# Two more weight-chunk slots from a halved DMA scratch, and conditioning chunks taken two at a time

## The chip, the cores and the metric

The kernel runs on one core of one Trainium2 chip. The metric is the device time of one execution in microseconds. Several executions of each kernel are taken on the same chip; their median stands for the kernel. One further execution was recorded by the hardware profiler, and all rows below come from it.

## The reference

One layer of a hybrid decoder trunk (D = 2048), for 256 prompt tokens and 8 × 4 sample tokens, 288 columns in all. All data and weights are fp32. Cut to what matters here:

```python
def block(x, c, st_pool, st_conv, st_ssm, st_ffn, pos0, lp):
    mod = silu(c) @ lp['w_ada'] + lp['b_ada']
    sh1, sc1, g1, sh2, sc2, g2 = [m[:, None] for m in jnp.split(mod, 6, axis=-1)]
    h = rmsnorm(x, lp['norm1']) * (1 + sc1) + sh1
    proj = h @ lp['w_in']
    u_pool, z, xbc, dt_raw = jnp.split(proj, [...], axis=-1)
    pool_out, new_pool = pool_mixer(u_pool, st_pool, pos0, lp['pool_w'], lp['pool_scale'])
    ssd_out, new_conv, new_ssm = ssd_mixer(z, xbc, dt_raw, st_conv, st_ssm, ...)
    mix = jnp.concatenate([pool_out, ssd_out], axis=-1) @ lp['w_out']
    x = x + g1 * mix
    h2 = rmsnorm(x, lp['norm2']) * (1 + sc2) + sh2
    ffn_out, new_ffn = conv_ffn(h2, st_ffn, lp['w_up'], lp['ffn_conv_w'], lp['ffn_conv_b'], lp['w_down'])
    x = x + g2 * ffn_out
    return x, new_pool, new_conv, new_ssm, new_ffn
```

The conditioning is the product of silu(c), for nine conditions (one prompt, eight samples), with w_ada; its first two parts, sh1 and sc1, shift and scale the first norm. A final norm follows the layer.

## The kernel before

**Weights.** All weights come from one flat tensor in HBM, cut into chunks of at most 128 × 1024 fp32 (512 KB) in the order of their use. `load` (line 211) puts the next chunk into a slot of the tag "raw" by a DMA on SyncE's queue; `RAW1 = 8` slots turn round, one more joins them late in the output projection (`RAW2`). A slot comes free when the last reader of its chunk is done, and the load waits for that.

**Three products for one.** A projection weight is split into a high part in fp32r (`whi`, ScalarE, line 217) and the rest (`wlo`, VectorE, line 218); two slots of each turn round. `mm3` then issues three TensorE matmuls of 128 × 128 weights by 288 columns: high by high (L223), high by low (L224), low by high (L225). `split` is the pair of copies.

**Conditioning.** `ada_group_units(gi)` computes sh1 and sc1 for K group `gi` of the model dimension. Its matmuls stay in plain fp32, with the nine conditions as weights (`sc_c`, 32 columns, four of them side by side in the array) and the chunk as the moving operand. The groups (`KGROUPS`: first K tile, number of K tiles) are (0,1), (1,1), (2,2), (4,4), (8,4) and (12,4): groups 0 and 1 take 4 chunks each, group 2 takes 8, groups 3 to 5 take 16 each. A chunk of group 2 is eight matmuls of 128 columns, one of groups 3 to 5 is four of 256 columns. At the end the sums are copied to SBUF (`asb`, ScalarE, L257), transposed on TensorE (`adat`, L263), and added to the bias (`ada`, VectorE, L309); `ada_scale` makes the multiplier (`amul`, L267). `modulate` then makes the group's operand: normalised rows times multiplier plus shift, VectorE for the prompt columns (L339, L342), POOL for the sample columns (L347, L348), and its split into `h1h` (ScalarE, L350) and `h1l` (VectorE, L351).

**Stages.** The input projection runs K group by K group: stage `gi` walks over 28 units (20 tiles of xBC, 2 of u, 6 of z), each a PSUM sum over that group's K tiles, which VectorE adds (L543) to the running sums `cvp`, `upp` and `zy`; stage 0 copies by ScalarE. Beside stage `gi` runs the conditioning of group `gi + 1`: it is a generator that issues one load, yields, and issues that chunk's matmuls when it is resumed. The main loop resumes it once per unit from unit `NX[gi]` on, and from unit 24 on drains it and calls `modulate`. In the last stage the mixers' steps (`back`) and the second conditioning (`adap`) are pulled in; the conv activation of a mixer is L573. Then come the remaining z and u tiles, the rest of the mixers, the output projection, the FFN's gate and value, and the down projection.

**Order.** Every engine runs its own queue in order. The order of each queue is made when the kernel is built: the framework orders the instructions by their dependencies and its own estimates of their times, and puts semaphore waits between engines. So the place of an instruction in the program is not its place in the queue.

**Scratch.** DMAs issued by POOL (queue q0 of the profile) use a scratch region in SBUF for their descriptors.

Of the kernel before, what the change touches and what calls it, by code (L numbers as in the profile page):

```python
# [19 lines left out]
KT = D // P  # L20
# [15 lines left out]
ET = XT + len(UEARLY) + 3 * ZEARLY  # L36
EPS = 1e-6
WU = (14, 2, 2, 2, 6)
RAW1, RAW2 = 8, 1
SPLIT1, SPLIT2 = 2, 2  # L40
YK = 2
NX = (10, 1, 1, 1, 1)
AY = 2

RA1, RA2, RB1, RB2, RB3 = 0.5, 0.4, 1.0, 1.0, 1.0
# [44 lines left out]
def _halves(nk):  # L90
    return [(0, 8), (8, nk - 8)]
# [40 lines left out]
def kernel(ctx: ExitStack, tc, ins, outs):  # L132
    nc = tc.nc
# [8 lines left out]
    def aux(name):  # L142
        return px.tile([P, 512], F32, tag="aux", name=name)
# [18 lines left out]
    ada = kp.tile([P, 6, KT, NC9], F32, name="ada")  # L162
# [8 lines left out]
    def warm_pe(n, rhs=None):  # L171

        for _ in range(n):
            nc.tensor.matmul(wps[:, :P], ones, ones if rhs is None else rhs, start=True, stop=True)
# [33 lines left out]
    def load(key):  # L208
        off, cols = S.items[key]
        t = wp[0].tile([P, RAWC], F32, tag="raw", name="raw_" + "_".join(map(str, key)))  # L210
        nc.sync.dma_start(t[:, :cols], wflat[off:off + P * cols].rearrange("(p n) -> p n", p=P))
        return t

    def split(raw, a, n, name):
        hi = wp[0].tile([P, RAWC], F32R, tag="whi", name="whi_" + name)
        lo = wp[0].tile([P, RAWC], F32R, tag="wlo", name="wlo_" + name)
        nc.scalar.copy(hi[:, :n], raw[:, a:a + n])  # L217
        nc.vector.tensor_tensor(lo[:, :n], raw[:, a:a + n], hi[:, :n].bitcast(F32), ALU.subtract)  # L218
        return hi, lo

    def mm3(ps, whi, wlo, c, bh, bl, first, last, n=P):
        w = slice(c * n, c * n + n)
        nc.tensor.matmul(ps, whi[:, w], bh, start=first, stop=False)  # L223
        nc.tensor.matmul(ps, whi[:, w], bl, start=False, stop=False)  # L224
        nc.tensor.matmul(ps, wlo[:, w], bh, start=False, stop=last)  # L225
# [23 lines left out]
    def ada_mm(ps, raw, k, c0, nb, js):  # L249
        for j in js:  # L250
            c = c0 + (j - js[0]) * nb
            nc.tensor.matmul(ps[32 * j:32 * j + 32, :nb], sc_c[:, k, :], raw[:, c:c + nb],  # L252
                             start=(k == 0), stop=(k == KT - 1), tile_position=(0, 32 * j))

    def ada_sb(ps, nb, name, r=P):
        asb = kp.tile([P, 512], F32, tag="asb", name="asb_" + name)
        nc.scalar.copy(asb[0:r, :nb], ps[0:r, :nb])  # L257
        return asb

    def ada_tr(asb, nb, name, r=P):  # L260
        pt = aux("adat_" + name)
        for i in range(nb // P):
            nc.tensor.transpose(pt[:, i * r:(i + 1) * r], asb[0:r, i * P:(i + 1) * P], ident[0:r, 0:r])  # L263
        return pt

    def ada_scale(which, part, norm, k0, gk):
        nc.vector.scalar_tensor_tensor(  # L267
            out=amul[:, which, k0:k0 + gk, :], in0=ada[:, part, k0:k0 + gk, :], scalar=1.0,
            in1=norm[:, k0:k0 + gk].unsqueeze(2).to_broadcast([P, gk, NC9]),
            op0=ALU.add, op1=ALU.mult)  # L270

    def ada_group_units(gi):

        k0, gk = KGROUPS[gi]
        nj = min(2 * gk, 4)
        nb = 2 * gk * P // nj
        per = RAWC // (nj * nb)
        ps = pa.tile([P, 512], F32, tag="ada", name=f"adag{gi}")
        for q in range(KT // per):
            raw = load(("ada", gi, q))  # L280
            yield
            if gk == 1:

                for kk in range(0, per, 2):
                    k = q * per + kk
                    for j in range(4):
                        nc.tensor.matmul(ps[32 * j:32 * j + 32, :nb], sc_c[:, k + j // 2, :],
                                         raw[:, kk * 256 + j * P:kk * 256 + j * P + P],
                                         start=(k == 0), stop=(k == KT - 2), tile_position=(0, 32 * j))
                if gi == 0 and q < WU[3]:  # L290
                    warm_pe(WU[2], raw[:, 0:P])
                continue
            for kk in range(per):
                ada_mm(ps, raw, q * per + kk, kk * nj * nb, nb, range(nj))
        r = 32 * nj
        if gk == 1:
            asb = ada_sb(ps, nb, f"g{gi}")
            pt = aux(f"adat_g{gi}")
            nc.tensor.matmul(pt[:, :r], asb[:, :nb], early[:, K_S2:K_S2 + r], start=True, stop=True)
            if gi == 0:  # L300
                warm_pe(WU[4], asb[:, 0:P])
        else:
            pt = ada_tr(ada_sb(ps, nb, f"g{gi}", r), nb, f"g{gi}", r)
        for i in range(nb // P):

            o = ada[:, 0:2, k0:k0 + gk, :].rearrange("p a (b i) c -> p a b i c", b=nj // 2)[:, :, :, i, :]
            b = bada[:, 0:2, k0:k0 + gk].rearrange("p a (b i) -> p a b i", b=nj // 2)[:, :, :, i]
            src = pt[:, i * r:(i + 1) * r].rearrange("p (a b c) -> p a b c", a=2, b=nj // 2)[:, :, :, 0:NC9]
            nc.vector.tensor_tensor(o, src, b.unsqueeze(3).to_broadcast([P, 2, nj // 2, NC9]), ALU.add)  # L309
        ada_scale(0, 1, early[:, V_N1:V_N1 + KT], k0, gk)  # L310

    def ada_part_units(part, ay=1):
        ps = pa.tile([P, 512], F32, tag="ada", name=f"adap{part}")
        for k in range(KT):
            raws = [load(("adap", part, k, h)) for h in range(2)]
            for h in range(2):
                ada_mm(ps, raws[h], k, 0, 512, range(2 * h, 2 * h + 2))
            if k % ay == ay - 1:
                yield
        asb = ada_sb(ps, 512, f"p{part}")  # L320
        yield
        pt = ada_tr(asb, 512, f"p{part}")
        for i in range(4):
            o = ada[:, part].rearrange("p (j i) c -> p j i c", j=4)[:, :, i, :]
            b = bada[:, part].rearrange("p (j i) -> p j i", j=4)[:, :, i]
            src = pt[:, i * P:(i + 1) * P].rearrange("p (j c) -> p j c", j=4)[:, :, 0:NC9]
            nc.vector.tensor_tensor(o, src, b.unsqueeze(2).to_broadcast([P, 4, NC9]), ALU.add)
        if part == 4:
            ada_scale(1, 4, vec[:, V_N2:V_N2 + KT], 0, KT)
        yield  # L330
# [54 lines left out]
    def xav(k0, gk):  # L385
        return xa[k0 // 4][:, k0 % 4:k0 % 4 + gk, :]
# [159 lines left out]
    def drain(gen):  # L546
        for _ in gen:
            pass
# [247 lines left out]
    def chain(*gens):  # L796
        for gn in gens:
            yield from gn

    adas = chain(*(ada_part_units(p, AY) for p in (2, 3, 4)))  # L800
    drain(ada_group_units(0))
    modulate(xav(0, KGROUPS[0][1]), rstd1p, 0, 0, 0, KGROUPS[0][1], "g0")
    conv0 = conv_group(0)
# [35 lines left out]
    def pull(gn, rate):  # L839

        credit[id(gn)] = credit.get(id(gn), 0.0) + rate
        while credit[id(gn)] >= 1:
            credit[id(gn)] -= 1
            next(gn, None)

    for gi in range(len(KGROUPS)):
        last = gi + 1 == len(KGROUPS)
        if last:
            hi, lo = split(load(("dt",)), 0, KT * NH, "dt")
            ps = pm.tile([P, 512], F32, tag="mm", name="mm_dt")  # L850
            for k in range(KT):
                mm3(ps[0:NH, :N], hi, lo, k, xhi[0][k], xlo[0][k], k == 0, k == KT - 1, NH)
            dt_stage(ps)
        else:
            if gi == 1:
                nc.sync.dma_start(vec, ins["vec"])
            if gi == 4:
                late_loads()
            nxt = ada_group_units(gi + 1)
            k0, gk = KGROUPS[gi + 1]  # L860
        for i, m in enumerate(xbc_units(gi)):
            if not last:
                if i >= NX[gi]:
                    next(nxt, None)
                if i == ET - 4:
                    drain(nxt)
                    modulate(xav(k0, gk), rstd1, 0, 0, k0, gk, f"g{gi + 1}")
            else:
                pull(back, 0.5 if m < 20 else RB1) if m >= 9 else None
                pull(adas, RA1 / AY)  # L870

# [3 lines left out]
    for m in list(range(4 + 3 * ZEARLY, 16)) + ULATE:  # L875
        for _ in uz_units(m):
            n += 1
            for gn in late.values():
                pull(gn, 0.5)
            pull(adas, RA2 / AY)  # L880
            pull(back, RB2 if n <= zlast else RB3)
# [3 lines left out]
        if m < 4:  # L885
            late[m] = pool_units(m)
            next(late[m])
    pull(adas, TA / AY)
    for h, (_, n) in enumerate(_halves(KT)):
# [69 lines left out]
    for m in range(16):  # L959
# [9 lines left out]
        squares(m, "a")  # L969
        pull(adas, (1 + (m >= 14 - ADA_OUT)) / AY)  # L970
        if m == 13:
# [260 lines left out]

# [27 lines left out]
```

## Time and profile before

| what | value |
|---|---|
| median of 3 runs | 1397.7 us (1396.01 to 1397.77) |
| the profiled execution | 1395.98 us |
| its span, first to last instruction | 1394.2 us |
| mean granted TensorE clock | 0.997 |
| HBM read / written | 309.78 MB / 10.39 MB, 230 GB/s over the span |
| loads of conditioning chunks (`raw_ada`) | 64 of 512 KB, 5.5 us from issue to landing (median) |
| loads of projection chunks (`raw_xbc`) | 55 of 512 KB, 5.9 us |

A row of a timeline reads: start and length in us, engine, line of the kernel, operation, output tile <- input tiles, shape, how many instructions it stands for, and in brackets the idle time of the engine before it with what ended it. A fp32 matmul of the conditioning leaves two records, so one chunk of four matmuls is a row of x8. The lengths of TensorE rows overlap, since matmuls are pipelined; the distance from one start to the next is the time that counts. PE is TensorE, DVE VectorE, ACT ScalarE, POOL GpSimd, SP SyncE; a name with q is the engine's queue.

### The profile page before, as it was taken

Reading aid. Unit: us, or ns where it says so; the run is one execution under the profiler, and the core shown is the slowest. Engines: PE = TensorE matmul, PEld = TensorE weight load, DVE = VectorE, ACT = ScalarE, POOL = GpSimd, SP = SyncE. Lnnn points to the kernel's source line nnn. Section 1 sums busy time; section 2 is a strip of 40 time slices with the busy share of each in tenths; the row PEclk is TensorE's granted clock in tenths of the full one; section 3 lists DMA queues with packets and bytes.
Section 4 is the critical chain, followed back from the end, with each engine's and each line's share of the span. In section 5 each row is a group of like instructions: output and inputs, shape, how many; then the busy total and the mean of one; then the engine's idle time right before and its main releaser. Section 6 shows DMA issues by size and latency. Waiting matters only on the chain.

```text
span 1394.2 us, 26416 instructions
## 1 busy us (share of the span) xinstructions
PE 1374.9 (99%) x10565; PEld 1253.5 (90%) x10565; DVE 822.3 (59%) x1409; ACT 577.0 (41%) x925; POOL 259.8 (19%) x466
## 2 busy tenths in 40 slices
PE   8999999999999999999999999999999999999997
PEld 7777888776668998989999999999999999999997
DVE  3775666867465446845665445666664466666553
ACT  5322333466673334533443333444343344444452
POOL 0000000344332222211211000221220011122221
PEclk9999999999999999999999999999999999999999
DMA  8889886867869886688655555655555555555631
GB/s 339 313 318 316 294 287 248 338 248 289 321 228 354 319 313 244 215 287 296 210 185 181 164 172 181 207 184 186 176 180 169 180 190 189 192 188 193 194 118 68
DMA packets 97196, 323.20 MB, mean 232 GB/s; under 512 B 10737, under 2 KB 19889, under 8 KB 97073
## 3 DMA queue, kind: packets, MB, share of 16 engines
q1 hardware_dynamic: 93168, 310.63, 64.8%
q0 software_dynamic: 3184, 9.69, 2.0%
q8 instruction: 83, 1.36, 0.4%
q10 hardware_dynamic: 720, 1.19, 0.2%
q14 instruction: 41, 0.33, 0.1%
HBM read 309.78 MB, written 10.39 MB: 230 GB/s over the span
## 4 chain that ended last, share of the span: by engine, by line
PE 70%; DVE 1%; issue 0%; ACT 0%; POOL 0%; DVEq 0%; POOLq 0%; ACTq 0%
PE mm_down L223 7%; PE mm_down L225 7%; PE mm_down L224 7%; PE mm_gate L225 6%; PE mm_gate L223 6%; PE mm_val L224 6%; PE mm_gate L224 6%; PE mm_val L225 6%; PE mm_val L223 6%; PE mm_out L223 3%; PE mm_out L224 2%; PE mm_out L225 2%; PE adap L252 2%; PE mm_up L223 1%; PE mm_up L224 1%; PE mm_up L225 1%
## 5 line engine op out<-in xcount | busy, mean ns | idle before, releaser
L223 PE MATMUL mm_down<-ah,whi_down 128*128 128x288 f32 x688 | 203.7, 296 | 0.0
L225 PE MATMUL mm_down<-ah,wlo_down 128*128 128x288 f32 x688 | 203.5, 296 | 0.0
L224 PE MATMUL mm_down<-al,whi_down 128*128 128x288 f32 x688 | 203.3, 295 | 0.0
L225 PE MATMUL mm_gate<-h2h,wlo_gate 128*128 128x288 f32 x640 | 190.2, 297 | 0.0
L223 PE MATMUL mm_gate<-h2h,whi_gate 128*128 128x288 f32 x640 | 189.8, 297 | 0.0
L224 PE MATMUL mm_gate<-h2l,whi_gate 128*128 128x288 f32 x640 | 189.3, 296 | 0.0
L224 PE MATMUL mm_val<-h2l,whi_val 128*128 128x288 f32 x640 | 188.8, 295 | 0.0
L225 PE MATMUL mm_val<-h2h,wlo_val 128*128 128x288 f32 x640 | 188.5, 295 | 0.0
L223 PE MATMUL mm_val<-h2h,whi_val 128*128 128x288 f32 x640 | 188.0, 294 | 0.0
L218 DVE TENSOR_TENSOR wlo_gate<-raw_gate,whi_gate 128x1024 fp32r<-128x1024 f32 x80 | 98.4, 1232 | 140.5 <-ACT whi_gate L217 140.3
L218 DVE TENSOR_TENSOR wlo_down<-raw_down,whi_down 128x1024 fp32r<-128x1024 f32 x96 | 108.2, 1127 | 116.0 <-ACT whi_down L217 115.1
L217 ACT CAST whi_down<-raw_down 128x1024 fp32r<-128x1024 f32 x96 | 92.2, 961 | 168.8 <-PE mm_down L224 120.3
L217 ACT CAST whi_gate<-raw_gate 128x1024 fp32r<-128x1024 f32 x80 | 83.8, 1050 | 168.3 <-PE mm_gate L224 76.2
L223 PE MATMUL xbc<-h1h,whi_xbc 128*128 128x288 f32 x448 | 139.1, 312 | 2.4 <-ACT h1h L350 1.3
L217 ACT CAST whi_val<-raw_val 128x1024 fp32r<-128x1024 f32 x80 | 84.1, 1051 | 127.8 <-issue 101.0
L224 PE MATMUL xbc<-h1l,whi_xbc 128*128 128x288 f32 x448 | 132.2, 296 | 0.0
L225 PE MATMUL xbc<-h1h,wlo_xbc 128*128 128x288 f32 x448 | 130.5, 298 | 0.6 <-DVE wlo_xbc L218 0.5
L224 PEld LDWEIGHTS mm_down<-al,whi_down 128*128 128x128 f32 x688 | 129.7, 189 | 0.0
L225 PEld LDWEIGHTS mm_down<-ah,wlo_down 128*128 128x128 f32 x688 | 129.6, 188 | 0.0
L223 PEld LDWEIGHTS mm_down<-ah,whi_down 128*128 128x128 f32 x688 | 129.6, 188 | 0.0
L223 PEld LDWEIGHTS mm_gate<-h2h,whi_gate 128*128 128x128 f32 x640 | 120.4, 188 | 5.0 <-ACT ah L1025 4.2
L224 PEld LDWEIGHTS mm_gate<-h2l,whi_gate 128*128 128x128 f32 x640 | 120.6, 189 | 0.0
(321 smaller groups left out, 3043.1 us busy)
## 6 DMA issues: line engine op xcount, KB each, us to landing
raw_adap<-wflat SPq DMA_DIRECT2D x128, 512.0 KB, 4.9
raw_gate<-wflat SPq DMA_DIRECT2D x80, 512.0 KB, 3.7
raw_val<-wflat SPq DMA_DIRECT2D x80, 512.0 KB, 3.5
raw_ada<-wflat SPq DMA_DIRECT2D x64, 512.0 KB, 5.5
raw_xbc<-wflat SPq DMA_DIRECT2D x55, 512.0 KB, 5.9
raw_down<-wflat SPq DMA_DIRECT2D x48, 512.0 KB, 3.6
raw_out<-wflat SPq DMA_DIRECT2D x32, 512.0 KB, 7.0
raw_down<-wflat SPq DMA_DIRECT2D x32, 384.0 KB, 3.1
```

What stands on the lines that cost most here:

```text
L217: nc.scalar.copy(hi[:, :n], raw[:, a:a + n])
L218: nc.vector.tensor_tensor(lo[:, :n], raw[:, a:a + n], hi[:, :n].bitcast(F32), ALU.subtract)
L223: nc.tensor.matmul(ps, whi[:, w], bh, start=first, stop=False)
L224: nc.tensor.matmul(ps, whi[:, w], bl, start=False, stop=False)
L225: nc.tensor.matmul(ps, wlo[:, w], bh, start=False, stop=last)
L252: nc.tensor.matmul(ps[32 * j:32 * j + 32, :nb], sc_c[:, k, :], raw[:, c:c + nb], start=(k == 0), stop=(k == KT - 1), tile_position=(0, 32 ...
```

## The change

Three edits. `RAW1` becomes 10: two more slots for chunks, 4 KB per partition each. The scratch of dynamic DMAs is set to 8192 bytes per partition, half of its default, which is where the room comes from. From K group 2 on (`gk > 1`), the conditioning issues the loads of two chunks at one visit and all their matmuls at the next, and the main loop resumes it at every second unit: 4 visits instead of 8 in stage 1, and 8 instead of 16 in stages 2, 3 and 4. The first and last unit with a visit stay as they were, as do the number and shape of all instructions. Groups 0 and 1 keep one chunk per visit.

```diff
-RAW1, RAW2 = 8, 1
+RAW1, RAW2 = 10, 1
...
+AG = 2
...
-        for q in range(KT // per):
-            raw = load(("ada", gi, q))
+        at = 1 if gk == 1 else AG
+        for q0 in range(0, KT // per, at):
+            raws = [load(("ada", gi, q)) for q in range(q0, q0 + at)]
             yield
-            if gk == 1:
+            for q, raw in zip(range(q0, q0 + at), raws):
+                if gk > 1:
+                    for kk in range(per):
+                        ada_mm(ps, raw, q * per + kk, kk * nj * nb, nb, range(nj))
+                    continue
...
                 if gi == 0 and q < WU[3]:
                     warm_pe(WU[2], raw[:, 0:P])
-                continue
-            for kk in range(per):
-                ada_mm(ps, raw, q * per + kk, kk * nj * nb, nb, range(nj))
...
-                if i >= NX[gi]:
+                if i >= NX[gi] and (gk == 1 or (i - NX[gi]) % AG == 0):
                     next(nxt, None)
...
-    nc = _bacc.Bacc("TRN2", target_bir_lowering=False, num_devices=1)
+    nc = _bacc.Bacc("TRN2", target_bir_lowering=False, num_devices=1, dynamic_dma_scratch_size=8192)
```

The main loop's `gk` is that of the group whose conditioning is under way, so stage 0 (conditioning of group 1) is as before.

## The prediction

> **What bounds the kernel now.** I read the page first, then a table of stretches, then timelines of TensorE and ScalarE at the places that the diff touches.
>
> ```profile
> span 1394.2 us, 26416 instructions
> PE 1374.9 (99%) x10565; PEld 1253.5 (90%) x10565; DVE 822.3 (59%) x1409; ACT 577.0 (41%) x925; POOL 259.8 (19%) x466
> ```
>
> TensorE is the bound of the whole; 577 us of ScalarE and 822 us of VectorE matter only where they make it wait. The stretches are the stages: K groups 1, 2, 3 and 4 of the input projection end near 55, 92, 150 and 210 us, the mixers near 425.
>
> ```profile
> core 0: us, PE busy (x) PEld busy (x) DVE busy (x) ACT busy (x) POOL busy (x), PEclk, DMA share, GB/s
> 25.00:55.00 30.00, 29.78 (x335) 22.78 (x333) 16.82 (x50) 15.26 (x52) 1.11 (x4) 1.00 0.86 303
> 55.00:92.00 37.00, 36.47 (x290) 25.80 (x282) 26.93 (x78) 8.37 (x10) 2.85 (x2) 1.00 0.90 325
> 92.00:150.00 58.00, 58.00 (x474) 49.11 (x475) 38.53 (x88) 18.13 (x24) 2.84 (x7) 1.00 0.85 299
> 150.00:210.00 60.00, 60.00 (x491) 50.63 (x490) 34.65 (x79) 16.63 (x21) 0.99 (x2) 1.00 0.87 297
> 210.00:425.00 215.00, 209.78 (x1579) 152.35 (x1577) 147.54 (x284) 125.27 (x250) 74.03 (x101) 0.99 0.77 283
> 425.00:1394.00 969.00, 959.72 (x7221) 936.11 (x7219) 548.58 (x815) 383.12 (x552) 176.13 (x343) 1.00 0.61 203
> ```
>
> From 425 us on TensorE issues 7221 matmuls in 969 us, 134 ns each, with the DMA at 0.61: nothing that the change touches can be late there. The case is decided before 425 us, where TensorE idles 0.75 us in the first two rows and 5.2 in the fifth (215 − 209.78). Busy time is not the same as useful time, though: a switch between kinds of matmul counts as busy. That is where pairing can pay.
>
> **Pairing, on TensorE.** One conditioning chunk is four fp32 matmuls (two records each) between projection matmuls. First one chunk, then two that stand together already:
>
> ```profile
> 173.81 0.29 PE L225 MATMUL xbc<-h1h,wlo_xbc 128*128 128x288 f32 x1
> 174.03 0.64 PE L252 MATMUL adag<-raw_ada,sc_c 128*32 128x256 f32 x8
> 174.60 0.40 PE L223 MATMUL xbc<-h1h,whi_xbc 128*128 128x288 f32 x1
> 174.84 0.30 PE L224 MATMUL xbc<-h1l,whi_xbc 128*128 128x288 f32 x1
> ```
>
> ```profile
> 76.69 0.30 PE L225 MATMUL xbc<-h1h,wlo_xbc 128*128 128x288 f32 x1
> 76.92 1.07 PE L252 MATMUL adag<-raw_ada,sc_c 128*32 128x256 f32 x16
> 77.92 0.40 PE L223 MATMUL xbc<-h1h,whi_xbc 128*128 128x288 f32 x1
> 78.16 0.30 PE L224 MATMUL xbc<-h1l,whi_xbc 128*128 128x288 f32 x1
> ```
>
> Without a visit two projection matmuls take 2 × 0.133 us (174.84 would follow 173.81 by 0.266). One chunk makes it 1.03, two make it 1.47: 0.765 and 1.205 us. So a visit costs 0.325 us for the two switches and 0.44 for each round of four matmuls, and a clean pair saves 0.325. A round is paid whole even when it is not full:
>
> ```profile
> 91.37 0.62 PE L252 MATMUL adag<-raw_ada,sc_c 128*32 128x256 f32 x2
> 91.92 0.40 PE L223 MATMUL xbc<-h1h,whi_xbc 128*128 128x288 f32 x1
> ```
>
> One matmul takes 0.55 us from start to the next projection matmul, four take 0.57 (174.03 to 174.60).
>
> If all 28 pairs came out clean, 28 × 0.325 = 9.1 us would go. They don't: the framework orders instructions by its own estimates, and in the order of the two built kernels the 64 matmuls of each K group stand in these visits. Group 5: sixteen visits of 4 become eight of 8, 16 × 0.765 − 8 × 1.205 = −2.60 us. Group 4: sixteen visits with 17 rounds become twelve with 19, −4 × 0.325 + 2 × 0.44 = −0.42. Group 3: nineteen with 21 become seventeen with 23 (two bunches of 15 at the end), −0.65 + 0.88 = +0.2. Group 2 has chunks of eight matmuls at half the width, so 0.22 a round: eight visits with 17 rounds become six with 18, −0.65 + 0.22 = −0.43. **Sum −3.25 us**, not 9.1; the bounds are 0 and −9.1, and I take −3.25, because it is counted from the order that will run.
>
> **What bunching makes late.** Each group's last conditioning matmul releases a chain: asb_g (ScalarE), transpose (TensorE), ada and amul (VectorE), scaling of h_g (VectorE, POOL L347 and L348), h1h (ScalarE). In the new order the last bunch comes ahead of projection matmuls, so the chain's ScalarE and VectorE parts come ahead of weight splits that TensorE needs at once. At the end of stage 1 the old rows are:
>
> ```profile
> 42.61 1.05 ACT L217 CAST whi_xbc<-raw_xbc 128x1024 fp32r<-128x1024 f32 x1 [3.35 <-DMA raw_xbc<-wflat]
> 48.34 0.27 ACT L257 COPY asb_g<-adag 128x128 f32<-128x128 f32 x1 [4.68 <-PE adag L252]
> 48.50 1.05 ACT L217 CAST whi_xbc<-raw_xbc 128x1024 fp32r<-128x1024 f32 x1
> 46.31 1.22 DVE L218 TENSOR_TENSOR wlo_xbc<-raw_xbc,whi_xbc 128x1024 fp32r<-128x1024 f32 x1
> 48.70 0.28 PE L263 MATMUL adat_g<-early,asb_g 128*128 128x128 f32 x1
> 49.30 0.37 PE L223 MATMUL xbc<-h1h,whi_xbc 128*128 128x288 f32 x1 [0.18 <-DVE cvp L543]
> ```
>
> The split of 42.61 was ready five us ahead of asb_g. Now it stands behind asb_g on ScalarE. All 32 remaining matmuls end at about 47.1; asb_g, then the transpose (0.36 behind it, as 48.34 to 48.70) at 47.5; the split 47.4 to 48.4; projection matmuls with its high part from 48.5; its low part, 1.22 us on VectorE behind amul and two scalings, to 49.95; the low matmuls from 50.0. What started at 49.30 starts at about 51.0: **+1.7 us**. Lower bound −0.3 (only the visits count, the split hidden), upper +2.3 (the low part also waits for POOL's use of VectorE's operands).
>
> At the end of stage 2 ScalarE's order in the old kernel is split, asb_g, three splits, four h1h. It becomes asb_g, split, two h1h, split, two h1h, split; on VectorE three scalings precede the low part. Old rows, and the same chain one group later, where POOL had less beside it:
>
> ```profile
> 85.40 0.37 ACT L257 COPY asb_g<-adag 128x256 f32<-128x256 f32 x1 [4.00 <-PE adag L252]
> 85.50 0.30 PE L225 MATMUL xbc<-h1h,wlo_xbc 128*128 128x288 f32 x1
> 87.32 0.29 PE L223 MATMUL xbc<-h1h,whi_xbc 128*128 128x288 f32 x1
> 89.33 0.40 PE L225 MATMUL xbc<-h1h,wlo_xbc 128*128 128x288 f32 x1 [0.53 <-DVE wlo_xbc L218]
> 91.98 0.40 DVE L342 TENSOR_SCALAR h_g<-h_g,amul,ada 128x256 f32<-128x256 f32 x1
> 88.19 1.36 POOL L347 TENSOR_TENSOR h_g<-h_g,amul 128x128 f32<-128x128 f32 x1 [37.26 <-DVE cvp L543]
> 89.63 1.49 POOL L348 TENSOR_TENSOR h_g<-h_g,ada 128x128 f32<-128x128 f32 x1
> 139.19 0.58 POOL L347 TENSOR_TENSOR h_g<-h_g,amul 128x128 f32<-128x128 f32 x1 [48.08 <-DVE cvp L543]
> 139.85 0.42 POOL L348 TENSOR_TENSOR h_g<-h_g,ada 128x128 f32<-128x128 f32 x1
> 140.31 0.77 ACT L350 CAST h1h<-h_g 128x288 fp32r<-128x288 f32 x2 [3.18 <-POOL h_g L348]
> ```
>
> Conditioning ends at 84.0, transposes 84.6, the split behind asb_g 85.4, its low part (behind ada, amul and three scalings of 0.40, so from 86.3) 87.5: the low matmuls of 85.50 start at 87.5. The next split waits behind two h1h, and these behind POOL's two operations, 1.0 us by the rows at 139 and 2.85 by those at 88; with the shorter its low part ends at 89.6 and the matmul of 87.32 starts at about 90.2. That is +2.9, less some 0.8 for the stall at 89.33, which goes, and its neighbours: +2.1 by the short rows, +3.9 by the long ones. In the new order L347 falls beside the scalings and only L348 beside a subtraction, so I go a third of the way: **+2.7 us**, bounds +1 (the splits overlap better) and +3.9.
>
> [...]
>
> Stage 3 ends with a split moved ahead of the first h1h instead of behind it, and stage 4 in the old order: 0, as TensorE was busy all 58 and 60 us there and the splits lead their use; bounds ±0.5.
>
> **Slots and scratch.** The splits hold the slots until the subtraction has run; two more let loads start earlier by two releases. What can this buy? Over 25 to 210 us TensorE idles 0.75 us in all, so a late DMA can have cost it no more there; where ScalarE waited for one (3.35 us at 42.61), VectorE came to the same chunk only at 46.31. Each projection chunk is now issued behind two conditioning chunks, one place later, which costs it 1.3 us (512 KB at the 404 GB/s below), and the extra slots pay that back: 0, bounds −0.7 (the few short waits behind 210 us) and +2.6 (1.3 us at each of the two ends above).
>
> ```profile
> 15.00:20.00 5.00, 4.61 (x74) 3.91 (x72) 1.32 (x5) 1.61 (x3) 0.01 (x1) 1.00 1.02 404
> q0 software_dynamic: 3184, 9.69, 2.0%
> ```
>
> The scratch serves POOL's own DMAs, queue q0: 2.0% of the engines' time, spread over the run; 0, upper bound +1. The queue of SP gets the same loads in nearly the same order; state loads that stand some twenty places later there are needed 70 us after.
>
> **Behind the groups** one reordering shows. ScalarE now does two splits ahead of a conv activation:
>
> ```profile
> 272.23 1.28 ACT L573 ACTIVATE cf<-cf 128x1280 f32<-128x1280 f32 x1 [8.94 <-DVE cf L563]
> 273.41 1.03 ACT L217 CAST whi_xbc<-raw_xbc 128x1024 fp32r<-128x1024 f32 x1
> 274.49 0.40 PE L223 MATMUL xbc<-h1h,whi_xbc 128*128 128x288 f32 x1 [0.93 <-ACT whi_xbc L217]
> ```
>
> The 0.93 us at 274.49 should go; bounds −1.0 and +1.0 (the activation's readers, later by two splits). I take −0.9. The mixers' transposes are regrouped in equal numbers: 0, ±1.
>
> **Sum:** −3.25 + 1.7 + 2.7 − 0.9 = **+0.25 us** on 1396.0, the profiled execution's own time (span 1394.2 and 1.8 around it). That lies 1.7 under the median of the runs, so the forecast is 1398.0.
>
> **Rivals.** *No change worth measuring* is the forecast, 0.42, own range 1395 to 1400.8. *The ends are hidden* (0.26): ScalarE runs its chain in the shadow of bunched conditioning, so both prices are about zero: −3.25 − 0.9 − 0.8 (the stall of 89.33 goes too), some −5 on 1397.7, 1392.7. For it: TensorE lost only 0.75 us in all at these places before. Against: the dependencies above are in the order, and TensorE has nothing else queued. *The port chain* (0.27): POOL's operations take the longer prices at each group's end, h1h is late, splits behind h1h late too. Over my sum it costs 1.2 at stage 2, 0.6 at stage 1 (its bound) and about 1 at each of stages 3 and 4 (1.85 less the lead of their splits), and it decides once L347 and L348 together pass 2.5 us at more than stage 2: 0.25 + 3.8 = +4.05, 1401.8. The rows at 88.19 are for it; for stages 3 and 4 the short rows at 139 are against. *The pairs dissolve and the slots are idle* (0.05): 1397.7.
>
> **Numbers.** A measurement tells about 0.2%, 2.8 us, from no change. Faster by that: the second case nearly whole, 0.25. Slower: the third case and a tail of the first, 0.32. Within: 0.43. The range, 1392 to 1403, takes in both rivals; the forecast's own range is the narrower one above.
>
> **What would show it.** Conditioning visits at group 5 of x16 records, 1.2 us each, and 2.6 us less over that stage. At 47 to 51 and 84 to 91 us: asb_g ahead of the split on ScalarE and projection matmuls behind wlo_xbc with idle time; 1.7 and 2.7 us lost. No idle at 274. From 425 us on the same rows, moved. I am wrong on size if POOL L347 takes 1.4 us at several groups; wrong in kind if TensorE waits for raw_xbc DMAs, or if stages 1 and 2 end no later than before.

## The result, and the profile after

The changed kernel took 1401.07 us in the median of nine runs (1400.34 to 1402.53), the kernel before beside it 1397.68 us (1395.75 to 1398.44). The ratio is 1.0029 with a 95% interval of 1.0019 to 1.004: slower by some 3.4 us, just beyond the 2.8 us within which I had forecast it. 1398.0 was forecast; the measured time lies in the range, on the side of the slower rivals.

The head of the page and the table of stretches of the changed kernel, in the columns of the table of before:

```profile
span 1399.6 us, 26438 instructions
PE 1376.0 (98%) x10565; PEld 1258.2 (90%) x10565; DVE 823.9 (59%) x1409; ACT 576.8 (41%) x925; POOL 256.1 (18%) x466
```

```profile
25.00:55.00 30.00, 27.64 (x307) 22.55 (x307) 15.25 (x45) 15.00 (x52) 2.35 (x4) 0.92 0.91 340
55.00:92.00 37.00, 35.36 (x271) 23.49 (x270) 24.32 (x69) 6.53 (x9) 0.99 (x2) 0.98 0.78 278
92.00:150.00 58.00, 56.71 (x463) 48.38 (x464) 38.09 (x89) 17.14 (x23) 3.61 (x7) 1.00 0.85 304
150.00:210.00 60.00, 60.00 (x512) 54.02 (x511) 38.87 (x86) 18.57 (x22) 1.00 (x2) 1.00 0.80 285
210.00:425.00 215.00, 210.10 (x1575) 152.57 (x1574) 146.73 (x280) 124.52 (x250) 72.35 (x98) 0.98 0.77 282
```

Two columns of TensorE stand out in the first row: its busy time (29.78 became 27.64) and its granted clock (1.00 became 0.92). The clock is what the forecast did not look at. The stretch from 150 to 210 us shows the other side: 512 matmuls where there were 491.

The projection matmuls are the same ones, in the same sequence but for about 1% of the places, so the start of each can be compared between two profiles. The table gives the lag behind the profile of before, in us, worked out from the rows of these matmuls; columns are the starts in the profile of before, the last holds from 457 us to the end.

```
kernel                      22.06  62.62  95.86 152.71 216.01 285.80 340.60 457.61
changed                     -0.27   4.82   7.12   6.44   3.68   2.53   5.94   5.41
changed, second profile      0.08   4.19   7.38   6.70   3.94   2.78   4.82   4.30
slots alone                  0.18   0.19   0.20   0.18   0.18  -1.00   1.49   1.03
pairs alone                 -0.06   4.34   6.62   5.95   4.67   4.69   4.75   4.78
pairs from group 3          -0.36  -0.99   2.11   1.44  -1.33  -2.51   0.01  -0.51
pairs for 5, 8 slots        -0.14  -0.12  -0.12  -0.14  -0.96  -0.98  -0.80  -0.80
pairs for 5, 10 slots        0.02   0.01   0.01   0.00  -2.77  -3.92  -1.01  -1.51
pairs for 4 and 5            0.11   0.11   0.12   0.18  -2.59  -3.75  -1.75  -2.24
filled, stage 1              0.00   3.20   7.55   6.88   4.11   2.96   5.96   5.41
filled in part               0.35   6.03   8.31   7.64   4.87   3.72   5.69   5.14
filled, stages 1 and 2      -0.22   3.01   6.53   5.20   2.44   1.26   3.23   2.74
pairs for 5, 12 dummies      0.00  -0.02  -0.01  -0.02  -2.79  -3.96  -0.94   2.41
```

The changed kernel loses 5.1 us up to 62 us and 2.3 more by 96 us, at the end of stage 2; it gains 0.7 in stage 3, 2.8 in stage 4 and 1.2 near 274 us, and loses 2.9 among the mixers. At 62.62 it has made one visit of group 3 more than the kernel before (nine against eight, some 0.75 us); at 95.86 both have made all visits of group 3 and one of group 4. Single profiles differ by 1 to 2 us: that of before lies 1.7 us under its median, and the two of the changed kernel end 1.1 us apart.

Now the place of the loss. Timelines of the changed kernel at the end of stage 1: TensorE, then ScalarE, VectorE and POOL.

```profile
47.31 0.33 PE L264 MATMUL adat_g<-early,asb_g 128*128 128x128 f32 x1 [0.44 <-ACT asb_g L258]
48.25 0.40 PE L224 MATMUL xbc<-h1h,whi_xbc 128*128 128x288 f32 x1 [0.62 <-ACT whi_xbc L218]
50.04 1.09 PE L226 MATMUL xbc<-h1h,wlo_xbc 128*128 128x288 f32 x3 [0.73 <-DVE wlo_xbc L219]
51.67 0.58 PE L224 MATMUL xbc<-h1h,whi_xbc 128*128 128x288 f32 x1 [0.54 <-DVE cvp L548]
```

```profile
46.99 0.27 ACT L258 COPY asb_g<-adag 128x128 f32<-128x128 f32 x1 [8.01 <-PE adag L253]
47.15 1.05 ACT L218 CAST whi_xbc<-raw_xbc 128x1024 fp32r<-128x1024 f32 x1
50.18 0.76 ACT L355 CAST h1h<-h_g 128x288 fp32r<-128x288 f32 x2 [1.98 <-POOL h_g L353]
```

```profile
48.77 1.22 DVE L219 TENSOR_TENSOR wlo_xbc<-raw_xbc,whi_xbc 128x1024 fp32r<-128x1024 f32 x1
50.64 0.46 DVE L356 TENSOR_TENSOR h1l<-h_g,h1h 128x288 fp32r<-128x288 f32 x1 [0.65 <-ACT h1h L355]
51.02 1.37 DVE L548 TENSOR_TENSOR cvp<-cvp,xbc 128x256 f32<-128x256 f32 x6
```

```profile
48.23 0.47 POOL L352 TENSOR_TENSOR h_g<-h_g,amul 128x64 f32<-128x64 f32 x1 [13.99 <-ACT whi_xbc L218]
48.77 1.37 POOL L353 TENSOR_TENSOR h_g<-h_g,ada 128x64 f32<-128x64 f32 x1
90.49 0.58 POOL L352 TENSOR_TENSOR h_g<-h_g,amul 128x128 f32<-128x128 f32 x1 [40.35 <-DVE amul L268]
91.15 0.41 POOL L353 TENSOR_TENSOR h_g<-h_g,ada 128x128 f32<-128x128 f32 x1
```

The first three waits of TensorE come as forecast, down to the low part's matmuls at 50.04. The fourth does not: at 51.67 the next matmul waits for a PSUM buffer that VectorE empties, VectorE's adds (51.02) stand behind h1l, h1l behind h1h, and h1h behind POOL, whose second operation began with the subtraction of 48.77 and took 1.37 us. In the profile of before it had taken 0.30:

```profile
50.63 0.30 POOL L348 TENSOR_TENSOR h_g<-h_g,ada 128x64 f32<-128x64 f32 x1
```

So POOL's operation took 1.37 us beside the subtraction, and 0.41 for twice the columns at 91.15, done before the subtraction of 91.63 began. In the profile of before, POOL's two long operations at the end of stage 2 (1.36 us from 88.19, 1.49 from 89.63) ran beside two subtractions:

```profile
88.06 1.22 DVE L218 TENSOR_TENSOR wlo_xbc<-raw_xbc,whi_xbc 128x1024 fp32r<-128x1024 f32 x1
89.62 1.21 DVE L218 TENSOR_TENSOR wlo_xbc<-raw_xbc,whi_xbc 128x1024 fp32r<-128x1024 f32 x1
```

That the subtraction makes POOL slow rests on these rows; no run was made for it.

The granted clock of the changed kernel in stretches of 3.4 us, and of the kernel before at its one such place:

```profile
43.20:46.60 3.40, 3.40 (x100) 3.02 (x88) 1.28 (x6) 0.00 (x0) 0.00 (x0) 1.00 0.80 294
46.60:50.00 3.40, 1.66 (x19) 0.96 (x7) 2.24 (x5) 1.21 (x2) 1.70 (x2) 0.99 0.88 324
50.00:53.40 3.40, 2.82 (x10) 2.50 (x11) 2.26 (x9) 1.71 (x3) 0.14 (x1) 0.50 1.00 399
53.40:56.80 3.40, 3.40 (x13) 2.31 (x12) 2.71 (x9) 0.62 (x1) 0.00 (x0) 0.50 0.39 159
56.80:60.20 3.40, 3.40 (x23) 1.60 (x23) 1.18 (x3) 0.00 (x0) 0.00 (x0) 1.00 0.15 28
```

```profile
313.40:316.80 3.40, 0.93 (x5) 0.70 (x5) 3.40 (x9) 3.37 (x8) 1.13 (x3) 1.00 0.52 140
316.80:320.20 3.40, 3.29 (x15) 2.98 (x16) 3.40 (x10) 3.37 (x10) 0.57 (x1) 0.51 1.04 389
320.20:323.60 3.40, 3.40 (x33) 2.23 (x35) 0.83 (x2) 1.01 (x4) 1.44 (x3) 0.99 0.90 319
```

After a stretch in which TensorE is busy for 1.66 us of 3.4, its clock is halved for two such stretches, 6.8 us: 13 matmuls stand between 53.4 and 56.8, in busy time that looks full; the projection matmuls there start 0.24 us apart, where 0.13 is their distance at full clock. So the stall is paid twice, once as a wait and once as slow work behind it.

### The profile page after: what moved, and what is told of

It reads as the page before. It is cut to its first block, busy times and chain, and to the rows that moved or that the text cites. A ratio compares the mean times of both kernels' runs of the same rounds, so it can differ in the third digit from the quotient of the medians.

```text
span 1399.6 us, 26438 instructions
## 1 busy us (share of the span) xinstructions
PE 1376.0 (98%) x10565; PEld 1258.2 (90%) x10565; DVE 823.9 (59%) x1409; ACT 576.8 (41%) x925; POOL 256.1 (18%) x466
## 3 DMA queue, kind: packets, MB, share of 16 engines
q8 instruction: 83, 1.36, 0.4%
## 4 chain that ended last, share of the span: by engine, by line
PE 70%; DVE 1%; issue 0%; ACT 0%; POOL 0%; DVEq 0%; POOLq 0%; ACTq 0%
PE mm_down L224 7%; PE mm_down L226 7%; PE mm_down L225 7%; PE mm_gate L226 6%; PE mm_gate L224 6%; PE mm_val L225 6%; PE mm_gate L225 6%; PE mm_val L226 6%; PE mm_val L224 6%; PE mm_out L224 2%; PE mm_out L225 2%; PE mm_out L226 2%; PE adap L253 2%; PE mm_up L224 1%; PE mm_up L225 1%; PE mm_up L226 1%
```

## The experiments

Eleven runs. In the experiments the number of chunks per visit is given for each group (`AG` becomes a tuple, `at = AG[gi]`, and `AG[gi + 1]` in the main loop). Ratios are to the kernel before on the same chip.

**Slots and scratch alone, pairs alone.**

```diff
# slots alone: RAW1 = 10, scratch 8192
-AG = 2
+AG = (1, 1, 1, 1, 1, 1)
# pairs alone
-RAW1, RAW2 = 10, 1
+RAW1, RAW2 = 8, 1
-..., dynamic_dma_scratch_size=8192)
+...)
```

> Two more slots and the halved scratch alone; conditioning chunks one at a time as before. Theory A (the loss comes from the bunched conditioning: a stall at the end of stage 1 after which the granted clock is halved for some 7 us, worth +5.5 us by 55 us, and +1 at the end of stage 2, against -2.8 in stage 4): up to 210 us this run is as before within 0.3 us; the idle time at 274 us goes (-1.2) and the half clock near 317 us may last one or two spans of 3.4 us, so 1396.5 to 1400. Rival B (the slots, the later loads or the scratch cost it): 1401, late already before 210 us.

> Pairs from K group 2 on alone, with 8 slots and the default scratch. Theory A: +3.7 us at 210 us with the clock at half for 5 to 7 us behind the stall at 47 to 51, 274 us stalls as before, so 1400 to 1402. Rival B: 1395 to 1398, no half clock near 50 us.

Slots alone: 1396.82 us, ratio 1.0 (0.9991 to 1.0009). Pairs alone: 1400.78 us, 1.0033 (1.002 to 1.0046). The cost is the pairs'. The slots with the small scratch cost nothing that can be measured; in the table they change no matmul before 216 us by more than 0.02 us, then gain 1.2 us at 274 us and give 2.5 us back by 340 us.

**Where the pairs cost.**

```diff
# pairs from group 3 on, 10 slots and small scratch
-AG = 2
+AG = (1, 1, 1, 2, 2, 2)
```

> The changed kernel with group 2's conditioning one chunk at a time (pairs from group 3 on). Theory A: no stall at 47 to 51 us, clock 1.0 there, so 5 us less than the changed kernel: 1395.5 to 1397.5. If only the idle time and not the clock had cost (rival C: the half clock comes by chance, not from the stall), about 2 us less: 1399. Rival B: 1401.

1395.12 us, ratio 0.999 (0.9981 to 0.9999): 5 us or more under the changed kernel, as theory A said. By 62 us its lag is −0.99 where the changed kernel's is 4.82. So of what the changed kernel loses up to 96 us (7.4), some two thirds (5.1) is at one place, the end of stage 1; the end of stage 2 still takes 3.1 us here (−0.99 to 2.11), with the clock halved for 3.4 us from 87.4 on.

**What clean pairs gain.** Pairs for group 5 alone, once with 8 slots and the default scratch, once with 10 slots and the small one; then for groups 4 and 5.

```diff
-AG = 2
+AG = (1, 1, 1, 1, 1, 2)     # the last run: (1, 1, 1, 1, 2, 2)
```

> The kernel before with pairs for group 5 alone, 8 slots, default scratch. Theory A: the visits' price alone: sixteen of x8 records become eight of x16, -2.6 us, all of it between 150 and 210 us: 1395.1. Rival B: with 8 slots pairs have no loads ahead of them, 0 or a loss.

> Pairs for group 5 alone, with 10 slots and the small scratch. In its order the last stage's visits are all clean pairs (with 8 slots the last three were broken up): -2.6 us between 150 and 210 us, nothing lost at the ends of stages 1 and 2: 2.6 us under the kernel before, ratio 0.998. If the slots were idle: as with 8 slots, 0.9 us, ratio 0.9993.

> Pairs for groups 4 and 5, with 10 slots and the small scratch. Group 4's visits are fewer by some pairs too, and no group end moves ahead: 0.5 to 1.5 us less than with pairs for group 5 alone, ratio 0.997. If the small waits at the end of stage 3 cost what the visits save: the same as for group 5 alone, 0.998.

With 8 slots 1395.75 us, 0.9992 (0.9982 to 1.0002); with 10 slots 1394.35 us, 0.9978 (0.9968 to 0.9987). In stage 4 the first gains 0.8 us, the second 2.8. The TensorE timelines say why; with 8 slots, from 183 us on:

```profile
183.81 1.05 PE L253 MATMUL adag<-raw_ada,sc_c 128*32 128x256 f32 x10
187.64 0.64 PE L253 MATMUL adag<-raw_ada,sc_c 128*32 128x256 f32 x8
188.93 1.06 PE L253 MATMUL adag<-raw_ada,sc_c 128*32 128x256 f32 x14
```

and with 10 slots:

```profile
185.39 1.07 PE L253 MATMUL adag<-raw_ada,sc_c 128*32 128x256 f32 x16
189.76 1.07 PE L253 MATMUL adag<-raw_ada,sc_c 128*32 128x256 f32 x16
```

So the slots do matter, through the order: with two more, the pairs stay whole to the end of the stage; with 8, the last six chunks come in pieces (the rows of x10, x8 and x14 records among them), which makes ten visits with 18 rounds instead of eight with 16. Slots and scratch were always changed together. Groups 4 and 5 together gave 1394.30 us, 0.9983 (0.9975 to 0.9992), the same as group 5 alone: in its order group 4's chunks stand in 13 visits with 20 rounds instead of 16 with 17, so by the prices nothing is saved there. Both beat both kernels.

**Wait or clock.** Dummy matmuls (results unused) in the changed kernel where TensorE waits; the framework put them there and left every other engine's order alone. In the run that fills both stalls four ScalarE and 19 VectorE instructions moved as well, and some of TensorE's own.

```diff
# filled, stage 1; in part: without the second warm_pe
-            pt = ada_tr(ada_sb(ps, nb, f"g{gi}", r), nb, f"g{gi}", r)
+            asb = ada_sb(ps, nb, f"g{gi}", r)
+            if gi == 2:
+                warm_pe(3, raw[:, 0:P])
+            pt = ada_tr(asb, nb, f"g{gi}", r)
+            if gi == 2:
+                warm_pe(6, asb[:, 0:P])
# filled, stages 1 and 2: also for gi == 3, with 3 and 10
```

> The changed kernel with nine dummy matmuls of 128 columns at the end of stage 1: three between the last conditioning matmul and the transpose, six behind the transpose; everything else stands in the same order on every engine. They fill idle time and shorten none of the waits. Theory (idle TensorE lowers its granted clock, and the halved clock costs more than the idle time): clock 1.0 from 47 to 60 us, the low part's matmuls start at 50.0 as before, and 2 to 2.5 us come back: ratio to the kernel before 1.001 to 1.002. Rival (the waits alone cost it, the clock falls by chance): the clock still halves near 50 us and the ratio stays at 1.003 or above.

> The same with the first three dummy matmuls alone: some 0.7 us of the 2.3 us idle ahead of 50 us are filled. If the clock falls on the idle share of a stretch of about 3.4 us, this can go either way: clock kept as in the full filling (ratio 1.001 to 1.002), or halved for one such stretch instead of two (1.002 to 1.003).

> The changed kernel with dummy matmuls in both stalls: nine at the end of stage 1 as before, thirteen at the end of stage 2 (three, six and four). Theory (idle time twice over: the wait itself, and half clock behind it): the clock stays 1.0 from 25 to 150 us in the profile, what is left is the waits alone, some 3.2 us by 62 us and 1.3 more by 97 us, less 2.8 in stage 4: 1.5 to 2.5 us less than the changed kernel run beside it, ratio to the kernel before 1.0005 to 1.0015. Rival (the filling merely adds work): the same as the changed kernel or slower.

> The changed kernel once more, its instructions in the same order on every engine, for the comparison on the same chip: ratio to the kernel before 1.002 to 1.004. A second profile also shows whether the half clock falls at the same places: theory, near 50 us always or nearly so, near 92 us in some executions, since the stall there is as long.

Stage 1 filled: 1399.79 us, 1.002 (1.0011 to 1.0029). In part: 1400.78, 1.0024 (1.0013 to 1.0034). Both stages: 1399.19, 1.0018 (1.001 to 1.0027). The changed kernel once more, on the same chip as the last: 1400.35, 1.0029 (1.0018 to 1.0039). Stretches of the run with stage 1 filled, on the borders used above:

```profile
43.20:46.60 3.40, 3.40 (x89) 3.03 (x92) 1.47 (x6) 0.00 (x0) 0.00 (x0) 1.00 0.85 289
46.60:50.00 3.40, 3.40 (x45) 3.19 (x37) 1.80 (x5) 1.21 (x2) 1.24 (x2) 1.00 0.92 343
50.00:53.40 3.40, 2.17 (x14) 1.72 (x12) 2.74 (x11) 1.71 (x3) 0.59 (x1) 1.00 1.01 394
```

With the same waits and TensorE kept at work, the clock stays whole, although nine matmuls were added, and the lag at 62 us, less that at 22 us, is 3.2 us instead of the 4.1 and 5.1 of the changed kernel's two profiles. So the half clock there cost 1.9 us in the first profile, where it lasted 6.8 us, and 0.9 in the second, where it lasted 3.4. In the profile of the filled run the end of stage 2 then lost the clock, which it had kept in the first profile of the changed kernel. With both filled, and in the second profile of the changed kernel, the stretches of stages 1 to 3 are:

```profile
25.00:55.00 30.00, 28.74 (x329) 23.39 (x329) 16.01 (x49) 15.69 (x53) 2.35 (x4) 1.00 0.91 339
55.00:92.00 37.00, 37.00 (x299) 26.68 (x299) 24.38 (x66) 6.50 (x9) 2.06 (x2) 1.00 0.85 299
92.00:150.00 58.00, 56.32 (x468) 48.53 (x467) 38.12 (x91) 17.77 (x22) 2.84 (x7) 1.00 0.83 298
```

```profile
25.00:55.00 30.00, 27.20 (x309) 22.22 (x308) 15.10 (x44) 15.37 (x54) 2.35 (x4) 0.94 0.92 337
55.00:92.00 37.00, 34.72 (x272) 23.37 (x271) 25.05 (x71) 7.17 (x10) 0.99 (x2) 1.00 0.83 291
92.00:150.00 58.00, 57.73 (x461) 49.60 (x462) 37.40 (x89) 16.23 (x20) 3.61 (x7) 0.97 0.83 299
```

The clock is 1.00 throughout with the filling; without it 0.94 and 0.97. Near 50 us it fell in all four profiles without the full filling (the changed kernel twice, pairs alone, the part filling) and in neither of the two with it. That the idle time brings the clock down is thereby shown. In the medians the filling of both stalls gives 1.2 us back, below the 1.5 to 2.5 I expected, and the intervals overlap; stage 1 alone gave 1.3 for an expected 2 to 2.5. The dummies are not free: at stage 2 the lag grows by 3.5 us (3.01 to 6.53) with the clock kept, where the changed kernel's grew by 2.3 with the clock kept and by 3.2 with it halved for 3.4 us. The part filling kept 1.0 until 51.7 us and then lost it for 6.8 us, and cannot be told from the changed kernel.

**The half clock that was there before.** Dummy matmuls at the stalls near 312 and 315 us, on top of pairs for group 5 alone.

```diff
+                if (g, t, i) == (1, 1, 1):
+                    warm_pe(5, yo[:, 0:P])
...
+                    warm_pe(7, raw[:, 0:P])     # ahead of the first low-part matmul of z tile 12
```

> The kernel with pairs for group 5 alone, and twelve dummy matmuls at the stalls near 312 and 315 us (seven ahead of the first low-part matmul of one z tile, five between two broadcasts of the decay sums), where the kernel before has a half clock for 3.4 us too. Theory: clock 1.0 there, 1.7 to 3.4 us less than the kernel with pairs for group 5 alone, ratio 0.996 to 0.997. Rival: the clock falls all the same, and the ratio is that kernel's or worse, since twelve matmuls and some reordering behind them are added.

A miss: 1397.03 us, 1.0003 (0.9994 to 1.0012), 2.7 us worse than without. The mixers' order changed around the dummies, and one broadcast now waits by itself, with the clock at half behind it all the same, for 3.4 us instead of 6.8:

```profile
311.26 0.61 PE L700 MATMUL cse<-csr,selr 128*128 128x288 f32 x1 [3.46 <-DVE yo L684]
```

That is not where the 2.7 us went, though: at 340.60 us the run is level with the one without dummies (−0.94 and −1.01 in the table). The loss comes behind it, at a wait for ScalarE that the other run does not have, and at a second half clock after it:

```profile
354.17 0.31 PE L718 MATMUL y<-vec,yo 128*64 128x32 f32 x4 [1.89 <-ACT ec L706]
355.40:358.80 3.40, 3.40 (x21) 1.50 (x14) 0.82 (x1) 3.37 (x7) 0.38 (x1) 0.50 0.97 336
```

Whether the half clock near 315 us can be had back is left open.

## Why the prediction was near, and where it failed

The forecast was no measurable change, by four terms that cancel. The measured time is 0.3 us beyond the forecast's own range (1395 to 1400.8) and inside the wide one. That it lies there is owed to the width: that range takes in both rivals, and the median was missed by 3.1 us. The measured terms below sum to 5.7 us where the medians are 3.4 apart, mostly because the profile of before lies 1.7 us under its median; so some 2 us of them are chance of these profiles. Measured terms are from the lag table, first and second profile of the changed kernel.

| step of the sum | forecast, us | measured, us |
|---|---|---|
| group 5's visits (stage 4) | −2.60 | −2.77, −2.77 |
| group 4's visits and the end of stage 3 | −0.42 | −0.67, −0.67 |
| end of stage 1 with group 2's visits | +1.7 − 0.43 | +5.1, +4.1 |
| end of stage 2 with group 3's visits | +2.7 + 0.2 | +2.3, +3.2 |
| stall at 274 us | −0.9 | −1.15, −1.16 |
| mixers behind it | 0 ± 1 | +2.9, +1.5 |

**Pairing on TensorE: right.** 0.325 us for a visit and 0.44 for a round carried over; the order of the built kernel was the right thing to count, and 9.1 us would have been wrong by far.

**The end of stage 1: right in mechanism, mis-sized.** This is the step that failed: +1.7 − 0.43 was put down for it, and it took 5.1 and 4.1 us. The split and its low part came at the time given (50.04 for "from 50.0"). Missing were two things. First, the matmul of 51.67, which the forecast had at 51.0, waits for VectorE's adds, at the end of the chain over POOL; I had POOL and the subtraction in each other's way only in the upper bound (+2.3). Against 49.30 before, and with the profile's lead of 0.27, the wait is 2.6 us, above even that bound. Second, the granted clock: 1.9 us in the first profile and 0.9 in the second, by the run with stage 1 filled. The 0.6 us left over in both is about the price of the one visit of group 3 that stands ahead of this point. I treated idle time as worth itself, though the profile of before had a halved clock behind its stalls near 315 us.

**The end of stage 2: right in order, near in size.** It took 2.3 us where the clock held and 3.2 where it was halved for 3.4 us, against the 2.9 put down. POOL took the short prices of 0.58 and 0.41 us there, not the third of the way to the long ones, and the forecast's short rows give just 2.1 + 0.2. The order of waits was as described:

```profile
90.29 0.40 PE L224 MATMUL xbc<-h1h,whi_xbc 128*128 128x288 f32 x1 [0.51 <-ACT whi_xbc L218]
92.90 0.40 PE L226 MATMUL xbc<-h1h,wlo_xbc 128*128 128x288 f32 x1 [1.55 <-DVE wlo_xbc L219]
```

**274 us: right in place and size**, but it is the slots with the small scratch that moved it (slots alone: −1.18), not the pairs (pairs alone: +0.02). **Slots: right** in that no DMA was behind any of it, and that scratch and slots alone come to 0; what the forecast did not see is that whole pairs depend on them. **Mixers: missed**, beyond the ±1 put down. The 274 us gain is given back at the stalls that follow. With 10 slots the clock was halved there for 6.8 us in some profiles and for 3.4 in others; in the medians nothing of it is left. At the first of them TensorE waits for VectorE's low part 1.82 us instead of 1.44. The rows of the kernel before, then of the changed one:

```profile
313.29 1.21 DVE L218 TENSOR_TENSOR wlo_uz<-raw_uz,whi_uz 128x1024 fp32r<-128x1024 f32 x1
314.56 0.40 PE L225 MATMUL mm_uz<-h1h,wlo_uz 128*128 128x288 f32 x1 [1.44 <-DVE wlo_uz L218]
```

```profile
315.17 1.13 POOL L659 TENSOR_TENSOR hf<-hf,s 128x384 f32<-128x384 f32 x1
315.36 2.01 DVE L219 TENSOR_TENSOR wlo_uz<-raw_uz,whi_uz 128x1024 fp32r<-128x1024 f32 x1
317.43 0.40 PE L226 MATMUL mm_uz<-h1h,wlo_uz 128*128 128x288 f32 x1 [1.82 <-DVE wlo_uz L219]
```

The subtraction now begins while POOL is at `hf`, and takes 2.01 us instead of 1.21. So it does in every profile with 10 slots, and in none of the three with 8 (before, pairs alone, group 5 alone). That is 0.4 us of the loss; how the rest divides between the longer half clock and the new order was not tried.

**The rivals.** That the ends are hidden fell. The port chain was nearer in time (1401.8) than the forecast, but only half right: POOL's long price came at stage 1, not at stages 2 to 4.

## What to carry to other kernels

A wait on TensorE in the middle of dense work can cost more than its length: look at the granted clock in stretches of some 3 us around each stall of the profile, and add a price for what is slowed (here 0.9 us for 3.4 us at half clock and 1.9 for 6.8). Fewer switches between kinds of matmul were worth having here only where the bunch did not come ahead of work that the next matmuls need at once; that was the last group, and taking pairs there alone, with the two slots that keep them whole, gave 2.2 us, where pairs from group 2 on lost 3.4. Count a batching change from the built order, not from the loop.

## What the hardware showed that I had not expected

The granted clock fell to 0.50 without a stretch of full idleness: TensorE was busy for 1.66 us of the 3.4 before it in the changed kernel, with no single wait over 0.73 us, and 0.93 of 3.4 in the kernel before, with none over 1.44. It stayed at half for 3.4 or 6.8 us. Nearly the same stall at the end of stage 2 (idle 0.48, 0.51 and 1.55 us) kept the clock in one profile and lost it in the second (1.00 and 0.97 in the stretch 92 to 150).

In every profile the changes of the clock lie on a grid of 3.41 us (in the first of the changed kernel at 49.96, 56.79, 319.61 and 326.44 us: 2, 77 and 2 steps). Cut along that grid, the stall at the end of stage 2 falls into two stretches in the first profile and for the most part into one in the second, behind which the clock falls:

```profile
87.51:90.92 3.41, 2.42 (x32) 1.35 (x24) 1.08 (x6) 1.32 (x2) 0.43 (x1) 1.00 0.99 390
90.92:94.33 3.41, 1.86 (x15) 1.63 (x14) 3.24 (x5) 2.38 (x5) 0.56 (x2) 1.00 1.03 418
```

```profile
88.98:92.39 3.41, 1.35 (x9) 0.95 (x8) 3.13 (x8) 2.05 (x4) 0.99 (x2) 1.00 1.02 399
```

Over all 13 profiles, between 20 us and 1385 us, 19 stretches of this grid at full clock have TensorE busy for 1.73 us or less, and the clock was halved behind 18 of them (the other had 1.60). Six have 1.86 to 1.89, and it was halved behind three. With 1.98 or more it was never halved.

So half busy (1.73 us of 3.41) was not enough to keep the full clock. The two outcomes of the stall at the end of stage 2 go with its least busy stretch: 1.86 us in the first profile, which kept the clock, and 1.35 in the second, which lost it.
